# Nearest-neighbour upsampling on one core: the head of the load cut into four DMAs of 32 partitions

## The chip, the cores and the metric

The kernel runs on one core of a Trainium2 chip. The metric is the device time of one execution in microseconds (us). Before the change it is 197.5 us, the median of three runs (197.13 to 197.62). A profile of one execution gives the times of every instruction and, in its trace, of every DMA packet.

## The reference

The input `x` is a float32 tensor of shape 16 x 64 x 64 x 64 (16.78 MB). Each pixel is repeated twice along the rows and twice along the columns, so that the output is 16 x 64 x 128 x 128 (67.11 MB):

```python
for i in range(new_h):
    for j in range(new_w):
        result[:, :, i, j] = x[:, :, i // scale_factor, j // scale_factor].copy()
```

There is no arithmetic. What has to happen is 16.78 MB in and 67.11 MB out, and a fourfold copy in between.

## The kernel before

**Tiling.** The 65,536 rows of 64 floats are dealt out in order to 128 partitions, so that each partition has 512 rows (`R`), which lie in one piece of 128 KB in HBM. One tile, `mem`, holds the whole input (`xt`, 512 rows of each partition) behind a work area of `WF` elements. Partition p holds rows 512p to 512p+511 and writes the output rows that come from them.

**Loads.** Line 194 issues three loads on SyncE's queue (SP), each over all 128 partitions: rows 0 to 255 (64 KB for each partition), rows 256 to 479 (56 KB), and rows 480 to 511 (8 KB). A DMA appears in the trace as one packet for each partition, so 64 KB, 56 KB or 8 KB long, and a semaphore packet of 4 bytes on each of 16 DMA engines at its end. `begin_before_barrier` takes the first `EARLY` SP instructions of the body (they must be loads that wait for nothing) and puts them ahead of SP's part in the barrier that opens the program; with `EARLY = 1` that is the first load. The other two loads follow the barrier.

**Expansion and stores.** `rows` cuts the 512 rows into nine pieces of 40 to 64 rows. For piece n, VectorE (DVE, line 214) expands the first 9/16 of its rows and ScalarE (ACT, line 215) the rest, both with a broadcast access pattern that repeats each element twice and each row twice; line 216 stores the result with one DMA from SP's queue. The first piece has 52 rows, of which DVE takes 29 (128x7424 elements written) and ACT 23 (128x5888). Pieces lie by turns at the bottom of `mem` and just below the rows not yet expanded, so that a later piece overwrites input that has been used up.

**Order.** SP issues everything in program order: three loads, then nine stores. Each store waits for the DVE and ACT copies of its piece. The first store also waits by hand for `loads[-2]`, the last load but one, so that stores begin as the loads end. A copy waits for the load of its rows and for the store that read its place before. DMA semaphores are dealt out in turn from a set of eight, so a later DMA uses a semaphore again after an earlier one. `close_early` (semaphore clearing at line 120) rearranges the end so that only the last store's landing is waited for at the very end.

Of the kernel before, what the change touches and what calls it, by code (L numbers as in the profile page):

```python
# [6 lines left out]

EARLY = 1  # L10


def begin_before_barrier(nc):
# [5 lines left out]
    sp = mybir.EngineType.SP  # L19
    loads = [i for i in body.instructions if i.engine == sp][:EARLY]  # L20
    for load in loads:
# [132 lines left out]
@with_exitstack  # L154
def kernel(
    ctx: ExitStack,
    tc: tile.TileContext,
    x: bass.AP,
    scale_factor: int,
    out: bass.AP,  # L160
):
    nc = tc.nc
    nc.at_finalize(begin_before_barrier)
    nc.at_finalize(close_early)
    P = nc.NUM_PARTITIONS
    s = int(scale_factor)
    B, C, H, W = x.shape
    R = B * C * H // P
    fdt = x.dtype

    xp = x.rearrange("b c h w -> (b c h) w").rearrange("(p r) w -> p r w", p=P)
    op = out.rearrange("b c (h hd) w -> (b c h) (hd w)", hd=s).rearrange(
        "(p r) w -> p r w", p=P
    )

    rows = [52, 40, 52, 63, 52, 64, 63, 63, 63]
    GROW = s * s
    FREE = 79
    WF = FREE * GROW * W
    assert sum(rows) == R
    mem_pool = ctx.enter_context(tc.tile_pool(name="mem", bufs=1))
    mem = mem_pool.tile([P, WF + R * W], fdt, name="mem")
    xt = mem[:, WF:].rearrange("p (r w) -> p r w", r=R)

    cuts = [0, R // 2, R - 32, R]
    loads = [
        nc.sync.dma_start(out=xt[:, lo:hi], in_=xp[:, lo:hi])
        for lo, hi in zip(cuts, cuts[1:])
    ]

    def expanded(r0, r1):
        return (
            xt[:, r0:r1].unsqueeze(2).unsqueeze(4).to_broadcast([P, r1 - r0, s, W, s])  # L200
        )

    r0 = 0
    before = (0, 0)
    for n, k in enumerate(rows):
        size = k * GROW * W
        at = 0 if n % 2 == 0 else WF + r0 * W - size
        assert at >= before[1] or at + size <= before[0]
        before = (at, at + size)
        u = mem[:, at : at + size].rearrange(  # L210
            "p (k a w b) -> p k a w b", k=k, a=s, w=W
        )
        kv = k * 9 // 16
        nc.vector.tensor_copy(out=u[:, :kv], in_=expanded(r0, r0 + kv))  # L214
        nc.scalar.copy(out=u[:, kv:], in_=expanded(r0 + kv, r0 + k))  # L215
        store = nc.sync.dma_start(out=op[:, r0 : r0 + k, :], in_=u)  # L216
        if n == 0:
            tc.add_manual_dep(
                store.ins,
                loads[-2].ins.name,  # L220
                mybir.DependencyInfo(
                    mybir.DependencyClass.Sync, mybir.DependencyReason.DATA
                ),
                reason="stores begin as the loads end",
            )
        r0 += k
# [35 lines left out]
```

## Time and profile before

| what | value |
|---|---|
| median of three runs | 197.5 us (197.13 to 197.62) |
| profiled execution, first to last instruction (span); the profile gives it no other time | 195.8 us |
| between the span and the median | 1.7 us |
| DMA: bytes read and written | 16.78 MB and 67.11 MB, 428 GB/s over the span |
| DVE busy, nine copies | 69.6 us (36%) |
| ACT busy, nine copies and one table load | 51.4 us (26%) |

How to read it: a line of the span in slices gives the busy share of an engine in tenths for equal slices of time; with a window, the 40 slices cover the window. In the DMA view a packet's bytes are counted in the slice in which it begins, so that with long packets a burst in the GB/s row is a set of packets that begin, and the distance between two bursts is the time that one packet takes. The share behind a queue is the time its packets took, as a share of 16 DMA engines. The view of waits names for each instruction line what ended its idle time. Times count from the first instruction, which here is SP's issue of the first load.

### The profile page before, as it was taken

The page shows a single profiled execution, that of the slowest core. Times are in us where ns is not written, and L with a number is a line of the kernel's source. Part 1 is how long each engine was busy: PE and PEld are TensorE (multiplying, and loading weights), DVE is VectorE, ACT ScalarE, POOL GpSimd, SP SyncE. Part 2 cuts the span into 40 slices and gives each one's busy share as a digit, 9 for nine tenths or more (in the row PEclk, how much of TensorE's full clock was granted, in tenths as well). Part 3 has the DMA queues.
Part 4 walks back from the last instruction along what each step waited for, and adds up shares of the span by engine and source line. Part 5 has one row for each costly group of instructions (what it writes and reads, how often), then busy time and mean ns, then how long its engine had stood idle before and what let it go on. Part 6 is the DMA issues. An engine that isn't in the chain of part 4 may idle for free.

```text
span 195.8 us, 102 instructions
## 1 busy us (share of the span) xinstructions
DVE 69.6 (36%) x9; ACT 51.4 (26%) x10; POOL 0.2 (0%) x4
## 2 busy tenths in 40 slices
DVE  0000596000039289069007205930693079100000
ACT  2000558000036083064920005666000074000000
POOL 0000000000000000000000000000000000000000
DMA  9999889699899999999999899999999999999994
GB/s 428 428 428 428 375 375 562 288 462 522 348 442 410 513 402 468 402 422 422 422 422 522 348 522 428 428 428 428 422 422 422 422 422 435 474 488 488 435 422 211
DMA packets 1728, 83.89 MB, mean 428 GB/s; under 512 B 192, under 2 KB 192, under 8 KB 192
## 3 DMA queue, kind: packets, MB, share of 16 engines
q1 hardware_dynamic: 1728, 83.89, 99.3%
HBM read 16.78 MB, written 67.11 MB: 428 GB/s over the span
## 4 chain that ended last, share of the span: by engine, by line
DMA 67%; DVE 18%; issue 0%; DVEq 0%; SPq 0%
DMA out_dram<-mem 48%; DMA mem<-in_x_dram 19%; DVE mem L214 18%; DVEq L214 0%; SPq L216 0%
## 5 line engine op out<-in xcount | busy, mean ns | idle before, releaser
L214 DVE COPY mem<-mem 128x8960 f32<-128x8960 f32 (+3 forms) x9 | 69.6, 7738 | 97.8 <-DMA out_dram<-mem 75.9
L215 ACT COPY mem<-mem 128x7168 f32<-128x7168 f32 (+2 forms) x9 | 50.1, 5572 | 111.7 <-DMA out_dram<-mem 82.7
L215 ACT ACT_TABLE_LOAD x1 | 1.3, 1283 | 0.8 <-PEq L243 0.8
L243 POOL MEMSET const-bfloat16-1.0<- 128x1 bf16 x1 | 0.1, 101 | 0.0
L243 POOL MEMSET const-uint8-127<- 128x1 uint8 x1 | 0.1, 101 | 0.0
L243 POOL MEMSET const-float32-0.0<- 128x1 f32 x1 | 0.1, 98 | 0.2 <-issue 0.2
L243 POOL MEMSET const-float32-1.0<- 128x1 f32 x1 | 0.1, 98 | 0.0
## 6 DMA issues: line engine op xcount, KB each, us to landing
out_dram<-mem SPq DMA_DIRECT2D x4, 8064.0 KB, 28.4
out_dram<-mem SPq DMA_DIRECT2D x3, 6656.0 KB, 19.7
mem<-in_x_dram SPq DMA_DIRECT2D x1, 7168.0 KB, 38.0
out_dram<-mem SPq DMA_DIRECT2D x1, 5120.0 KB, 29.7
mem<-in_x_dram SPq DMA_DIRECT2D x1, 1024.0 KB, 40.1
mem<-in_x_dram SPq DMA_DIRECT2D x1, 21.8
out_dram<-mem SPq DMA_DIRECT2D x1, 29.9
```

Source lines behind the costliest of these rows:

```text
L214: nc.vector.tensor_copy(out=u[:, :kv], in_=expanded(r0, r0 + kv))
L215: nc.scalar.copy(out=u[:, kv:], in_=expanded(r0 + kv, r0 + k))
L243: nc = _bacc.Bacc("TRN2", target_bir_lowering=False, num_devices=1)
```

## The change

The load's first 32 rows of each partition (8 KB) are taken out of the first load and come in four DMAs of their own, each over 32 partitions: partitions 0, 4, 8, ... 124, then 1, 5, ... 125, and so on. The first wide load now has rows 32 to 255 (56 KB for each partition); the two others are as before. `EARLY` goes from 1 to 5, so that the four head loads and the first wide load stand ahead of the barrier. Nothing else is edited; `loads[-2]` still is the wide load of rows 256 to 479. In the changed file the loads are at lines 195 and 198, and the copies and stores at lines 218, 219 and 220.

```diff
-EARLY = 1
+EARLY = 5
...
-    cuts = [0, R // 2, R - 32, R]
+    HEAD, Q = 32, 4
+    cuts = [HEAD, R // 2, R - 32, R]
     loads = [
+        nc.sync.dma_start(out=xt[q::Q, :HEAD], in_=xp[q::Q, :HEAD]) for q in range(Q)
+    ]
+    loads += [
         nc.sync.dma_start(out=xt[:, lo:hi], in_=xp[:, lo:hi])
         for lo, hi in zip(cuts, cuts[1:])
     ]
```

## The prediction

> **What bounds the kernel now.** I read the page's span and DMA queue first, then the chain of waits, then the DMA view in short windows, and last the trace's DMA packets one by one. The page's queue line and its chain:
>
> ```profile
> q1 hardware_dynamic: 1728, 83.89, 99.3%
> ...
> DMA 67%; DVE 18%; issue 0%; DVEq 0%; SPq 0%
> ```
>
> The 16 DMA engines are taken for 99.3% of the span. The 18% that the chain gives to DVE are no idle time of the DMA: while DVE expands a piece, an earlier store is still moving. So the end is set by the bytes, and by the little that is not bytes: 0.7% of 195.8 us, or 1.4 us. It lies at the two ends. The DMA view of the first 5 us and of 10 to 15 us, in slices of 0.125 us:
>
> ```profile
> GB/s 0 0 0 0 0 0 0 0 4194 3146 524 524 0 0 0 0 0 0 0 0 0 0 0 0 0 0 0 0 0 0 0 0 524 2097 2621 1573 1573 0 0 0
> ```
> ```profile
> GB/s 0 0 0 0 0 0 0 0 0 0 1049 1573 2621 2097 1049 0 0 0 0 0 0 0 0 0 0 0 0 0 0 524 1573 2621 1049 2621 0 0 0 0 0 0
> ```
>
> In the first window nothing moves for 1.0 us; then 16 packets of 64 KB begin within four slices, and the next 16 begin about 3 us later. In the second window the distance between two bursts is about 2.4 us. The packets say it exactly. The first load's issue takes 0.383 us on SP. The first packets of the 16 engines begin at 1.009 to 1.478 us and take 3.02 to 3.39 us, so they end at 4.04 to 4.58. From then on each engine runs without a hole: 64 KB packets follow each other every 2.414 us, 56 KB every 2.113, 8 KB every 0.306, and a semaphore packet costs 0.006. From the end of its first packet to its last one each engine needs about 190.9 us. The span's end is therefore the end of the slowest start-up (4.576 us) plus that fixed train, plus some 0.35 us until the last semaphore is seen. **Whatever the change does to the start-up or to the train shifts the time one to one; what it does to DVE, ACT or SP counts only if a store comes late enough to empty the DMA queue.**
>
> **The change, part by part.** The sum is made against the profiled span of 195.8 us; the 1.7 us between it and the median of 197.5 I carry over.
>
> 1. *More packets.* Each engine's eight packets of 64 KB become eight of 8 KB and eight of 56 KB: 0.306 + 2.113 = 2.419 for 2.414 us, 8 x 0.005 = 0.04 us. Seven loads instead of three give four more semaphore packets for each engine: 4 x 0.006 = 0.024 us. Together **+0.06 us** on the path. It is measured on DMAs over 128 partitions; if packets of the narrow DMAs run otherwise, see the second rival.
>
> 2. *When the first packets begin.* A narrow DMA has 32 rows to describe, not 128. The trace has no narrow DMA, so I bound it. If nothing of the 1.478 us goes with the number of rows: 0. If the whole issue (0.383) and the whole spread of the beginnings (1.478 - 1.009 = 0.469) go with it, a quarter stays: -0.75 x 0.852 = -0.64 us for the last engine. Above nothing: the engines would run dry if narrow DMAs came too slowly. One narrow DMA feeds two packets to each engine, 2 x 0.306 + 0.006 = 0.618 us. The loads behind the barrier are issued in 0.332 and 0.424 us, the second 0.383 us after the first; that is faster than they are eaten. The longest distance between two load issues in the trace is 0.79 us (with the barrier between); at that pace 4 x (0.79 - 0.618) = +0.7 us would be lost. Bounds -0.64 to +0.7. The issue rows are all near 0.38 us for 8 KB and for 64 KB alike, so I leave the issue where it is and let half of the spread go: **-0.25 us**.
>
> 3. *How long the first packets take.* They take 0.60 to 0.97 us more than the 2.418 of the later ones. If this is a delay that is paid once whatever the packet's size, the gain is 0. If it goes with the packet's size (first packets run at 71 to 80% of the pace), an 8 KB packet pays an eighth, and 0.53 to 0.85 us are gained. If each of four narrow DMAs paid it again, it would cost up to 3 x 0.97 = 2.9 us; but the row that is nearest, the step from one load to the next on a running engine, shows 0.006 us (a 56 KB packet follows the semaphore packet at once). The train of equal packets after the first speaks for a delay paid once: **0**.
>
> 4. *SP's queue and the barrier.* Four head loads and the wide one are issued ahead of the barrier, and the barrier comes 4 x 0.33 to 4 x 0.42 = 1.3 to 1.7 us later. Behind it stand ACT's table load, the copies, and the last two loads, issued at 0.79 and 1.17 us before. The engines need the next load at about 21.2 us, where the wide load's packets end, so 18 us are spare. Cost 0; without that cover it would be the 1.7 us.
>
> 5. *ACT's table load.* In the built program the table load, which waited for nothing and ran at 0.79 us, now carries waits for three head loads and the wide load, and moves to 21.9 us, where ACT's first copy stood. What is behind it on ACT is the first two copies:
>
> ```profile
> 0.79 1.28 ACT L215 ACT_TABLE_LOAD   x1 [0.79 <-PEq L243]
> 21.86 5.10 ACT L215 COPY mem<-mem 128x5888 f32<-128x5888 f32 x1 [19.79 <-DMA mem<-in_x_dram]
> 21.86 10.89 DVE L214 COPY mem<-mem 128x7424 f32<-128x7424 f32 x2 [21.86 <-DMA mem<-in_x_dram]
> 29.84 4.03 ACT L215 COPY mem<-mem 128x4608 f32<-128x4608 f32 x1 [2.88 <-DVE mem L214]
> 38.86 128.88 SPq L216 DMA_DIRECT2D out_dram<-mem  x9
> ```
>
> The copy ends at 21.9 + 1.28 + 5.1 = 28.3, where ACT idled 2.88 us for DVE until 29.84: hidden. Even with all 1.28 us added to 33.87 there are over 3 us to the first store at 38.86, which waits for the load of rows 256 to 479. Cost 0.
>
> 6. *DVE's first copy.* Its 29 rows lie in the 32 of the head, so in the built program it waits for the four head loads alone and can begin near 5 us instead of 21.9. Nobody gains: the first store still waits for that later load, and DVE's second copy (rows 52 on) for the wide one. Gain 0.
>
> 7. *Stores.* They wait for the same loads; semaphores that are used again belong to DMAs long landed. At 38.8 us the last load (eight packets of 0.306 us on each engine) still runs, so the queue stays full for 2.4 us. Cost 0.
>
> Sum: +0.06 - 0.25 + 0 = -0.19 us; 195.8 becomes 195.6, and 197.5 becomes **197.3 us**. A measurement of this kernel tells some 0.3% (0.6 us) from no change, so the forecast counts as no change.
>
> [...] The trace charges a further DMA on a full queue 0.006 us an engine. [...]
>
> **Rivals.**
>
> *A. The start-up shrinks with the packet (faster).* Term 3 at its lower end. The engine that ends its start-up last (1.478 + 3.098) has 0.68 us of excess; seven eighths are 0.6. With term 2: -0.6 - 0.25 + 0.06 = -0.8 us, **196.7 us**, and 196.3 with term 2 at its end. For it: first packets of 16 engines differ by 0.37 us, as something shared would make them. Against it: the excess does not grow with a later start, and no row shows a short first packet.
>
> *B. The narrow DMAs run at a lower rate (slower).* Their packets may be dealt to the engines in another way than those of wide DMAs, so that two engines meet at one place in the memory and halve each other. Place: the 8 packets of 8 KB at the head. Price: at half rate 8 x 0.306 = +2.45 us; engines that begin 0.15 us apart, about a third of the spread, share only the other half of each packet: 8 x 0.15 = +1.2 us. With terms 1 and 2 about +1.0, **198.5 us**, up to 199.8. It decides once packets after the first take over 0.38 us on average (8 x 0.075 = 0.6 us). For it: no DMA with stepped partitions is in the trace. Against it: in all wide DMAs, loads and stores, all 16 engines hold the same pace.
>
> [...]
>
> *C. The change does not do what it says:* the narrow DMAs use fewer than 16 engines. With eight, those carry 16 packets of 8 KB instead of 8, +2.45 us: **199.7 us**. Nothing in the trace decides it.
>
> **How the numbers follow.** Forecast 0.47, with its own range 196.9 to 197.9 (term 2 from -0.64 to +0.3). A 0.26, B 0.23, C 0.04. So faster 0.26, same 0.47, slower 0.27. The range 196.4 to 199.0 takes in A almost whole and B at its likely price; some 0.06 of A and 0.1 of B and C with the far ends of terms 2 and 3 are left out.
>
> **What would show it.** In the changed profile: first packets of 8 KB that begin at about 1.0 to 1.3 us and take 0.9 to 1.3 us (A: 0.4), later head packets at 0.31 us (B: 0.4 to 0.6), engines without holes between the head loads; DVE's first copy near 5 us; ACT's table load behind the wide load; the first store still just after the load of rows 256 to 479, near 38.7 us. The forecast is wrong if the slowest engine has not moved the eight head packets (8 x 0.306 = 2.45 us of work, as much as the first 64 KB packet that ends at 4.576 us now) between about 4.0 and 4.9 us: earlier speaks for A, later for B or C, and a hole between packets for term 2's upper end.

## The result and the profile after

The changed kernel takes 200.39 us (median of four runs, 199.14 to 201.36) against 197.37 for the kernel before: 1.015 times the time, 95% interval 1.012 to 1.018. The forecast was 197.3 us with a range up to 199.0. The profiled execution took 199.14 us, the shortest of the four; its span is 197.8 us, 2.0 more than before, while the median is 3.0 more. What the longer runs have on top is read below from a second profile of the change.

The page's queue line, its chain, and three of its DMA issue lines (columns: count, KB each, median us from issue to landing):

```profile
q1 hardware_dynamic: 1920, 83.89, 98.8%
...
DMA 66%; DVE 18%; issue 0%; DVEq 0%; SPq 0%
...
out_dram<-mem SPq DMA_DIRECT2D x4, 8064.0 KB, 28.4
...
mem<-in_x_dram SPq DMA_DIRECT2D x2, 7168.0 KB, 29.1
...
mem<-in_x_dram SPq DMA_DIRECT2D x4, 256.0 KB, 3.8
```

The bytes are the same and the DMA still bounds the kernel, but its share falls from 99.3 to 98.8%. A narrow DMA of 256 KB takes 3.8 us to land, though it is 0.6 us of work for 16 engines. The DMA view of the first 5 us, to be laid beside the one of before:

```profile
GB/s 0 0 0 0 0 0 0 0 0 0 393 262 262 0 66 197 459 262 393 459 262 655 328 197 525 131 197 328 262 393 262 131 197 197 328 590 197 1442 131 524
```

Nothing moves for 1.25 us where it was 1.0. With packets this short the row reads as a rate from 2 us on, and its mean up to 4 us lies well below 428 GB/s. By whole microseconds (columns: stretch, length, DVE, ACT and POOL busy, clock, DMA share, GB/s):

```profile
1.00:2.00 1.00, 0.00 (x0) 0.00 (x0) 0.00 (x0) 1.00 0.69 147
2.00:3.00 1.00, 0.00 (x0) 0.00 (x0) 0.00 (x0) 1.00 0.95 377
3.00:4.00 1.00, 0.00 (x0) 0.00 (x0) 0.00 (x0) 1.00 1.08 279
```

From 2 to 4 us, while the head loads run, the engines move 279 to 377 GB/s. The timeline shows what else moved:

```profile
0.00 2.46 SPq L195 DMA_DIRECT2D mem<-in_x_dram  x4
...
2.50 1.91 SPq L198 DMA_DIRECT2D mem<-in_x_dram  x3
6.52 7.88 DVE L218 COPY mem<-mem 128x7424 f32<-128x7424 f32 x1 [6.52 <-DMA mem<-in_x_dram]
23.69 3.09 DVE L218 COPY mem<-mem 128x5632 f32<-128x5632 f32 x1 [9.28 <-DMA mem<-in_x_dram]
23.75 1.28 ACT L219 ACT_TABLE_LOAD   x1 [23.75 <-DMA mem<-in_x_dram]
25.05 9.16 ACT L219 COPY mem<-mem 128x5888 f32<-128x5888 f32 x2
40.69 129.00 SPq L220 DMA_DIRECT2D out_dram<-mem  x9
```

DVE's first copy and the table load stand where they were foreseen in the order, some 1.5 to 1.9 us later than foreseen (6.52 for near 5, 23.75 for 21.9). ACT is done at 34.2 us, and the first store still follows its load, only that it comes at 40.69 instead of 38.86. So 1.83 of the 2.0 us are lost before the first store, in the loads.

**One sum for all runs.** The trace's packets allow an account, as the mean over the 16 engines. A packet does not carry its engine's number; packets are joined to 16 chains by their ends and beginnings. *Begin* is when an engine's first packet begins. *Delay* is what packets of the loads took beyond the fixed length of their size (0.309 us for 8 KB, 2.116 for 56 KB, and so on). *Empty* is the time between an engine's packets in which it had none, up to its first packet of a store. *Stores* is what the store phase took beyond its packets. *Uneven* is how much later than the mean the last engine ends. Together with the *work* (all packets at their fixed pace) and 0.36 us to the end of the span they give the span to 0.04 us in every run, in us:

| run | work | begin | delay | empty | stores | uneven | span |
|---|---|---|---|---|---|---|---|
| before | 193.25 | 1.14 | 0.79 | 0.00 | 0.04 | 0.23 | 195.84 |
| the change | 193.31 | 1.49 | 1.41 | 0.46 | 0.27 | 0.47 | 197.79 |
| the change, again | 193.31 | 1.48 | 1.70 | 1.34 | 0.48 | 0.53 | 199.20 |
| b_early3 | 193.25 | 1.13 | 0.76 | 0.00 | 0.04 | 0.25 | 195.78 |
| m_step4 | 193.31 | 1.27 | 0.69 | 0.04 | 0.45 | 0.35 | 196.48 |
| m_wide | 193.30 | 1.16 | 0.79 | 0.06 | 0.43 | 0.31 | 196.45 |
| m_cont | 193.31 | 1.17 | 3.24 | 0.00 | 0.05 | 0.27 | 198.37 |
| h_wide | 193.30 | 1.15 | 0.66 | 0.01 | 0.10 | 0.50 | 196.08 |
| c_8k | 193.35 | 1.14 | 0.82 | 0.10 | 0.39 | 0.23 | 196.41 |
| h_64 | 193.31 | 1.54 | 1.14 | 0.13 | 0.38 | 0.49 | 197.37 |
| h_128 | 193.32 | 1.50 | 0.68 | 0.04 | 0.35 | 0.44 | 196.70 |
| h_2x64 | 193.30 | 1.47 | 0.76 | 0.24 | 0.47 | 0.42 | 197.02 |
| h_4wide | 193.46 | 1.20 | 0.94 | 0.56 | 0.37 | 0.50 | 197.42 |
| h_cont | 193.31 | 1.23 | 2.48 | 0.04 | 0.05 | 0.20 | 197.69 |
| h_src | 193.31 | 1.46 | 1.44 | 1.49 | 0.50 | 1.05 | 199.60 |

For the change the rise is 0.06 (work) + 0.35 (begin) + 0.62 (delay) + 0.46 (empty) + 0.23 (stores) + 0.24 (uneven) = 1.96 us. In before no engine is ever empty after it has begun. In the change some are: after the 16 beginnings, nine more packets of the head and four 56 KB packets begin on an engine that had nothing queued, and most of them are delayed again, by up to 1.05 us (an 8 KB packet of 1.359 us).

Two of the columns hold more than one thing. Of the delay of 1.41 us in the change, 0.34 is in the 16 first packets and 0.3 to 0.4 in packets that begin on an empty engine; the remaining 0.6 to 0.7 is in packets of the first 10 us that follow another packet without a hole. And *empty* counts two places: the head, and the step from the last load to the first store. In the change nearly all of it is in the head (0.05 at the stores); in its repeat it is 0.62 in the head and 0.72 at the stores, in h_src 0.67 and 0.84, in h_4wide 0.28 and 0.31. In m_step4, m_wide, c_8k and h_128 all but 0.03 at most is at the stores.

### The profile page after: what moved, and what is told of

Same layout as the page of the kernel before. It is cut to its first block, busy times and chain, and to the rows that moved or that the text cites. A ratio compares the mean times of both kernels' runs of the same rounds, so it can differ in the third digit from the quotient of the medians.

```text
span 197.8 us, 111 instructions
## 1 busy us (share of the span) xinstructions
DVE 69.7 (35%) x9; ACT 51.4 (26%) x10; POOL 0.2 (0%) x4
## 3 DMA queue, kind: packets, MB, share of 16 engines
q1 hardware_dynamic: 1920, 83.89, 98.8%
## 4 chain that ended last, share of the span: by engine, by line
DMA 66%; DVE 18%; issue 0%; DVEq 0%; SPq 0%
DMA out_dram<-mem 47%; DMA mem<-in_x_dram 19%; DVE mem L218 18%; DVEq L218 0%; SPq L220 0%
```

## The experiments

The kernels differ from the kernel before or from the change only in the loads. Ratios are against the kernel before on the same chip, with 95% intervals.

**m_step4, m_wide, m_cont: the head in the middle of the queue.** The wide load of rows 32 to 255 goes first (`EARLY = 1`), then the head, then the last two loads:

```diff
+    loads = [nc.sync.dma_start(out=xt[:, HEAD : R // 2], in_=xp[:, HEAD : R // 2])]
+    for q in range(4):                                       # m_step4
+        nc.sync.dma_start(out=xt[q::4, :HEAD], in_=xp[q::4, :HEAD])
...
+    nc.sync.dma_start(out=xt[:, :HEAD], in_=xp[:, :HEAD])    # m_wide, in place of the four
...
+        p = slice(32 * q, 32 * q + 32)                       # m_cont, xt[p] and xp[p] in the four
...
```

> The same seven loads as in the change, but in another order: the wide load of rows 32 to 255 goes first (alone ahead of the barrier, as before the change), the four narrow head loads follow it, then the two last wide loads. So the narrow DMAs are issued while each engine still has some 15 us of queued work. Theory S (supply: the narrow DMAs cost because SP issues them slowly at the start, 0.62 us apart, and the engines begin late and run dry) expects nothing but the 0.06 us of the extra packets: span 195.9 (195.8 to 196.1) and head packets of 0.309 us. Theory P (path: packets of a 32-partition DMA are dealt so that two engines meet at one place and slow each other) expects head packets of 0.4 to 1.4 us here too and a span 1 to 2.5 us longer than before, 196.8 to 198.3.

> As m_step4, but the head is one wide DMA of 8 KB for each of 128 partitions in place of four narrow ones. Control for the cut into more and smaller packets: both theories expect 8 KB packets of 0.309 us and a span of 195.8 to 196.0.

> As m_step4, but each narrow DMA takes 32 neighbouring partitions (0 to 31, 32 to 63, and so on) instead of every fourth. Theory S: nothing, 195.9. Theory P: if the packets are dealt in pairs by their order, neighbouring engines now write neighbouring partitions through the same place all the time, and no packet of theirs can slip past: head packets near twice 0.309 us throughout, span 2 to 2.6 us longer, 197.8 to 198.5.

Measured: m_step4 197.81 us, ratio 1.002 (1.001 to 1.003); m_wide 197.78 us, 1.002 (1.001 to 1.003); m_cont 199.66 us, 1.012 (1.010 to 1.013). The stretches from 19 to 21 us in m_step4, then from 19 to 22 in m_cont:

```profile
19.00:20.00 1.00, 0.00 (x0) 0.00 (x0) 0.00 (x0) 1.00 1.02 426
20.00:21.00 1.00, 0.00 (x0) 0.00 (x0) 0.00 (x0) 1.00 1.04 434
```
```profile
19.00:20.00 1.00, 0.14 (x1) 0.00 (x0) 0.00 (x0) 1.00 1.18 279
20.00:21.00 1.00, 1.00 (x1) 0.00 (x0) 0.00 (x0) 1.00 0.94 197
21.00:22.00 1.00, 1.00 (x1) 0.00 (x0) 0.00 (x0) 1.00 1.10 254
```

With work queued ahead, the stepped narrow DMAs moved at the full rate, 426 to 434 GB/s: all 128 packets of the head in m_step4 took 0.309 us, and m_step4 equals its wide control. Theory P falls for stepped partitions. For neighbouring partitions its price holds: in m_cont the packets fall into two groups, near 0.31 and near 0.6 us, the delay grows by 2.45 us over m_wide, and the head's 1.05 MB take 2.47 + 2.45 = 4.9 us, an estimated 213 GB/s. That two engines meet at one place is only the theory's reason for it; no run shows it. The spans of m_step4 and m_wide were 0.4 us above their expectations; the account puts that into *stores*, which no theory here foresaw.

**h_wide: the head first, but as one DMA** (`EARLY = 2`).

```diff
-        nc.sync.dma_start(out=xt[q::Q, :HEAD], in_=xp[q::Q, :HEAD]) for q in range(Q)
+        nc.sync.dma_start(out=xt[:, :HEAD], in_=xp[:, :HEAD])
```

> The change, but with the head as one wide DMA over 128 partitions in place of four narrow ones (EARLY is 2, so that the wide load of rows 32 to 255 still stands ahead of the barrier). Both theories expect the narrowness to be what costs, so a time near before: span 195.7 to 196.2. If 8 KB packets at the very start or a second issue ahead of the barrier are what costs, it is over 197.

Measured: 197.54 us, ratio 1.001 (1.000 to 1.002), span 196.1. Short packets at the very start and a second issue ahead of the barrier cost almost nothing; the first packets even cost a little less delay (0.66 for 0.79 us). It is the four DMAs.

**h_64, h_src, h_cont and the change again.** In h_64 `HEAD` is 64. In h_cont the partitions are `32 * q` to `32 * q + 31`. In h_src only the source is another:

```diff
+    flat = x.rearrange("b c h w -> (b c h) w").rearrange("(n p r) w -> n p r w", p=32, r=32)
-        nc.sync.dma_start(out=xt[q::Q, :HEAD], in_=xp[q::Q, :HEAD]) for q in range(Q)
+        nc.sync.dma_start(out=xt[q::Q, :HEAD], in_=flat[q]) for q in range(Q)
```

> The change with a head of 64 rows instead of 32: the same four stepped narrow DMAs, of 16 KB packets, and the first wide load that much shorter (48 KB packets). Theory S (supply): one narrow DMA now feeds each engine 1.23 us of work, twice the 0.62 us between two issues, so no engine runs dry after it has begun. What stays is the late first packet (1.3 to 1.9 us) and the first packet's own delay: span 196.0 to 196.5, and hardly any packet after an engine's first one over 0.64 us. Theory P2 (place: stepped narrow packets collide when the engines work in step, as they do at the start and not in the middle of the queue): twice the bytes collide, so at least the loss of the change, span 197.8 to 199.5.

> The change, but each narrow DMA reads one contiguous block of 256 KB of the input instead of 32 rows that lie 512 KB apart; the SBUF side is untouched. So the first 32 rows of each partition hold other data, and the output of those rows is not the reference's. If the slow packets of the change come from where the head is read in HBM, they go: span under 196.8. Theories S and P2 both put the cause elsewhere and expect the time of the change, span 197.5 to 200.

> The change with 32 neighbouring partitions in each narrow DMA instead of every fourth. In the middle of the queue these were issued in 0.35 to 0.43 us (stepped ones 0.53 to 0.61) but half of their packets took twice 0.309 us. So here the first packets should begin near 1.0 us again and no engine should run dry (0.4 us to issue, 0.62 or more to move), and the time should be before plus the 2.4 us that the neighbours cost: span 198.0 to 198.6. If the slow issue were not what makes the first packets late in the change, they begin at 1.3 us or later here too.

> The change once more, unedited: its four runs fell at 199.1, 199.5, 201.3 and 201.4 us, and the profile shows one of the lower ones. Expected 199.0 to 201.5. If this profile is of a longer run, it shows which part of the start-up or of the stores the further 2 us are in: theory S expects them in the head (engines that run dry and start anew), before the first store.

Measured: h_64 198.85 us, ratio 1.009 (1.007 to 1.011); h_src 199.63 us, 1.012 (1.007 to 1.018); h_cont 199.06 us, 1.009 (1.007 to 1.011); the change again 200.55 and 199.59 us, ratio 1.015 (1.012 to 1.017).

h_src is as slow as the change: where the head lies in HBM is not the cause. The repeated change shows what its longer runs are made of: between its two profiles the span grows by 1.41 us, of which 0.88 are empty time and 0.29 delay. Only some 0.2 of the 0.88 are in the head; the rest is at the first store. Before, that store was issued at 38.86 us, while all engines still had packets of the last load; in the repeat one engine began a 56 KB packet only at 7.14 us after 2 to 4 us of nothing, the store had to wait for the latest engine and was issued at 42.25, and 14 of the 16 engines were out of work when its first packets came at 43.1. Before, from 39 to 40 us, and the repeat, from 42 us:

```profile
39.00:40.00 1.00, 0.00 (x0) 0.00 (x0) 0.00 (x0) 1.00 1.04 442
```
```profile
42.00:42.50 0.50, 0.00 (x0) 0.00 (x0) 0.00 (x0) 1.00 0.51 213
42.50:43.00 0.50, 0.00 (x0) 0.00 (x0) 0.00 (x0) 1.00 0.08 33
43.00:43.50 0.50, 0.00 (x0) 0.00 (x0) 0.00 (x0) 1.00 3.70 1556
```

So in the repeat the holes in the head left the engines apart, and a second hole followed near 42 us (0.72 us on the mean). h_cont began at 1.03 us, so the late beginning comes from the stepped shape: its narrow DMAs were issued in 0.39 to 0.42 us, the stepped ones in 0.55 to 0.59. It then lost to its neighbours (delay 2.48) and was hardly ever empty; the time fell 0.3 us under what was expected. h_64 fits neither theory: theory S expected 196.0 to 196.5 and P2 at least 197.8, and it came to 197.37. Of the 1.53 us that its span is over before, 0.40 are in the beginning and 0.35 in delay, 0.34 in the stores, 0.26 in uneven ends and 0.13 empty. Five packets of its third and fourth narrow DMA began on an empty engine, between 4.4 and 6.5 us, where those DMAs had been issued at 1.2 to 2.5. So the pace of the issues is not all: what is issued reaches single engines late.

**c_8k, h_2x64, b_early3: work ahead of the narrow DMAs, more work in each, more issues alone.**

```diff
+    cuts = [2 * HEAD, R // 2, R - 32, R]                                                # c_8k
+    loads = [nc.sync.dma_start(out=xt[:, :HEAD], in_=xp[:, :HEAD])]
+    loads += [nc.sync.dma_start(out=xt[q::Q, HEAD : 2 * HEAD], in_=xp[q::Q, HEAD : 2 * HEAD])
+        for q in range(Q)]                                                              # EARLY = 6
...
-    HEAD, Q = 32, 4
+    HEAD, Q = 32, 2                                                                     # h_2x64, EARLY = 3
...
-EARLY = 1
+EARLY = 3                                                                               # b_early3
```

> The head as one wide DMA of 8 KB packets (2.45 us of work for each engine, issued in 0.37 us), then four stepped narrow DMAs of 8 KB packets for the next 32 rows, then the rest wide; six loads ahead of the barrier. Every narrow DMA is now issued while wide packets are still queued, and each brings 0.62 us of work in 0.62 us. Theory S (supply): the first packets begin at 1.0 us again, no engine runs dry, and the time is that of the wide head plus the extra packets: span 196.0 to 196.5. Theory P2 (stepped narrow packets collide when engines work in step near the start): they collide here too, span 197 or more, with narrow packets well over 0.309 us that begin at once after the one before them.

> The change with two DMAs of 64 partitions (every second one) in place of four of 32: each brings 4 packets of 8 KB, 1.23 us of work for an engine, in one issue, and there are two issues fewer ahead of the wide load. Theory S: about as much supply as the 64-row head but 1.2 us less issuing, so no more loss than that one's 1.5 us: span 196.2 to 197.4. Theory P2: the same bytes through the same stepped pattern, so the loss of the change: 197.8 to 199.5.

> The kernel before with all three wide loads ahead of the barrier (EARLY is 3), nothing else. Tells what the later barrier and more issues at the start cost by themselves: expected nothing, span 195.7 to 196.0, since all that stands behind the barrier has some 18 us to spare. If more issues beside the first packets disturb them, the first packets take over 3.4 us and the span grows.

Measured: c_8k 197.82 us, ratio 1.003 (1.002 to 1.004); h_2x64 197.92 us, 1.003 (1.002 to 1.005); b_early3 197.20 us, 1.000 (0.999 to 1.001). In c_8k, by microseconds:

```profile
2.00:3.00 1.00, 0.00 (x0) 0.00 (x0) 0.00 (x0) 1.00 0.96 401
3.00:4.00 1.00, 0.00 (x0) 0.00 (x0) 0.00 (x0) 1.00 0.98 418
4.00:5.00 1.00, 0.00 (x0) 0.00 (x0) 0.00 (x0) 1.00 1.02 418
5.00:6.00 1.00, 0.00 (x0) 0.00 (x0) 0.00 (x0) 1.00 1.00 418
```

The same four stepped DMAs, issued just as slowly (0.54 to 0.61 us) and run from 3.5 us on, cost next to nothing behind 2.45 us of wide packets: empty 0.10 instead of 0.46 to 1.34, begin 1.14. P2 falls: stepped packets near the start are not slow in themselves (delay 0.82 us, for 0.79 in before). Two DMAs with four packets for each engine lose 0.6 us by the medians, where four with two lose 2.9 to 3.0. In b_early3 the later barrier and two further issues ahead of it cost nothing.

**h_4wide, h_128: shape or too little work.**

```diff
-        nc.sync.dma_start(out=xt[q::Q, :HEAD], in_=xp[q::Q, :HEAD]) for q in range(Q)
+        nc.sync.dma_start(out=xt[:, 8 * q : 8 * q + 8], in_=xp[:, 8 * q : 8 * q + 8]) for q in range(Q)  # h_4wide
...
-    HEAD, Q = 32, 4
+    HEAD, Q = 128, 4                                                                                      # h_128
```

> The head again in four DMAs and five loads ahead of the barrier, but each of the four is over all 128 partitions and 8 rows deep (2 KB packets, eight for each engine and DMA, at least 0.6 us of work). If the narrow, stepped shape is what delivers late (a wide DMA was issued in 0.37 to 0.42 us, a stepped one in 0.55 to 0.59), this one begins at 1.0 us and runs without holes: span 196.0 to 197.0, with a little for the 24 further packets on each engine. If four small DMAs in a row at the start are too little work whatever their shape, engines run dry here too: span 197.5 to 199.5.

> The change with a head of 128 rows: four stepped narrow DMAs of 32 KB packets, 2.45 us of work for each engine and DMA against 0.62 us between issues. With 64 rows some engines still ran dry, as packets of the fourth DMA began up to 4.7 us after its issue. Late delivery expects that 2.45 us of work covers this: empty time of the engines under 0.1 us on the mean, about 0.8 us of delay in the first packets, the late beginning at 1.3 to 1.9 us left over: span 196.3 to 196.9. If stepped narrow packets are slow in themselves near the start, four times the bytes of the change are slow: span 198 or more.

Measured: h_4wide 199.05 us, ratio 1.009 (1.006 to 1.013); h_128 197.92 us, 1.003 (1.002 to 1.004). The first microseconds of h_4wide:

```profile
1.00:2.00 1.00, 0.00 (x0) 0.00 (x0) 0.00 (x0) 1.00 0.81 248
2.00:3.00 1.00, 0.00 (x0) 0.00 (x0) 0.00 (x0) 1.00 0.96 342
3.00:4.00 1.00, 0.00 (x0) 0.00 (x0) 0.00 (x0) 1.00 1.15 348
```

It begins at 1.0 us and is issued every 0.42 to 0.47 us, faster than its 0.65 us of work for each DMA, and yet its engines are empty for 0.56 us (0.28 in the head) and move 342 to 348 GB/s. Its span, 197.42, is just under the range for engines that run dry. So the stepped shape makes the beginning late (1.46 to 1.54 us on the mean with four of them at the head, 1.20 here), but four small DMAs in a row at the start are too little work for wide ones too. Here the packets are also only 2 KB long, and no run tells that from the size of the DMA. h_128 came out as late delivery expects: 2.45 us of work for each DMA leaves 0.04 us empty and no packet of its loads but the first 16 on an empty engine. With 32, 64 and 128 rows in the head, empty and delay together fall from 1.87 (3.04 in the repeat) over 1.27 to 0.72 us, less than the 0.79 of before. What stays is the late beginning (1.50), with 0.35 in the stores and 0.44 in uneven ends.

No version here beats the kernel before.

## Why the prediction was wrong

1. *More packets, +0.06:* held. Work grows by 0.064 us, and in m_step4 the loads lose nothing else in sum that its control does not.
2. *When the first packets begin, -0.25:* wrong in sign; +0.35 was measured. I took the issue row of wide DMAs (0.38 us); a stepped one takes 0.55 to 0.59 us and its first packet begins at 1.33, not 1.01. **The step that failed is the sentence that issues are "faster than they are eaten".** They came every 0.61 to 0.64 us for 0.618 us of work, and the engines were empty for 0.46 us, 1.34 in the repeat. And the comparison itself was too simple, since h_4wide is issued faster than it is eaten and still runs empty: a mean pace does not tell when a single engine gets its packets. The end that I kept for this, +0.7, counted the empty time only, not the delay that engines paid when they began anew (up to 1.05 us).
3. *The first packet's delay, 0:* part of rival A is real, as 8 KB first packets were delayed by 0.34 us on the mean in the change, for 0.79 with 64 KB. But engines that ran empty paid again, packets that followed one another without a hole were slow as well, and the sum rose to 1.41 and 1.70. **The second step that failed:** I had a bound for paying again (up to 2.9 us) and dropped it for the step between two loads on a running engine. That row shows a full queue; the change makes a short or empty one, so it was not the nearest. The term stood at 0 and measured +0.62, in the repeat +0.91.
4. *Barrier, table load, DVE's first copy:* held at no cost, as the timeline and b_early3 show.
5. *Stores:* their order held. The cover of 2.4 us by the last load held nearly in the first profile (0.05 us empty) and not in the repeat (0.72), as it counted on engines that keep together; the sum had no term for engines that drift apart, and the uneven ends alone cost +0.24. The stores' packets also ran a little slower, 0.27 to 0.48 us in sum for 0.04 before. It comes with several variants (m_wide among them, which has no narrow DMA) and not with others (m_cont, h_cont). What sets it stays open.

Rival B had the right side, though 200.39 us is over its upper end of 199.8. The half rate that it priced was measured for neighbouring partitions (m_cont, packets near 0.6 us), not for every fourth (m_step4, 0.309 us); that two engines meet at one place in the memory, its reason, was not shown. Its mark, head packets over 0.38 us on the mean after the first ones, was met (0.40, and 0.42 in the repeat) for another reason: stepped packets with more work queued, in c_8k and h_128, are not slow, and h_4wide, with no narrow DMA, has 0.9 us of delay behind its first packets. Rival C is out: 256 semaphore packets for 16 DMAs are 16 engines each.

I priced a further DMA by a row of a full queue, 0.006 us an engine. In m_step4 and c_8k the row is right (0.04 and 0.10 us empty). At the head of an empty queue four DMAs cost begin, delay and empty of 1.4 to 2.6 us more than one wide load, 0.4 to 0.6 us for each. No run here shows the reason.

What is shown: in the change engines ran empty (0.46 us, 1.34 in the repeat) and mostly began anew with a delay (up to 1.05 us); the repeat lost again at the first store (0.72 us empty); more work in each DMA (h_128, 0.04 us empty, 0.68 delay) or work ahead of them (c_8k, 0.10 and 0.82) removed the holes in the head and the further delay; stepped partitions by themselves (m_step4, ratio 1.002), HBM addresses (h_src, as slow as the change at 199.63 us) and the barrier (b_early3, 1.000) did not cause them. What is only argued: that late and uneven delivery of packets to the engines is behind it. No view here shows a packet on its way between issue and engine. Why packets without a hole before them are slow in a short queue, 0.6 to 0.7 us in sum, stays open too.

## What to carry to other kernels

When DMA bounds a kernel, its first load should be one that gives every engine enough work until the next DMA has reached all of them. Here 2.45 us sufficed (c_8k, h_128) and 1.23 did not (h_64, h_2x64). Four small loads cut out of it left holes (0.46 us empty in the change, 1.34 in the repeat) that nothing hid: the spans grew by 2.0 and 3.4 us. Read the cost of a further DMA from a row with the same queue: what costs 0.006 us on a full one cost up to 0.6 us on an empty one. And where a change opens a stream, count every new beginning, not the first alone.

## What the runs showed of the hardware

- A DMA over stepped partitions was issued in 0.53 to 0.66 us (every fourth) or 0.57 to 0.58 (every second), and the wide load right behind one in 0.58 to 0.61. In kernels without stepped DMAs the loads, over neighbouring partitions or all 128, were issued in 0.33 to 0.53, most of them in 0.33 to 0.43.
- DMAs over 32 neighbouring partitions ran at half the rate, an estimated 213 GB/s from 1.05 MB in 2.47 + 2.45 us (m_cont); those over every fourth ran at 426 to 434 GB/s (m_step4).
- The delay of an engine's first packet, 0.5 to 1.0 us with 64 KB packets (before, b_early3), did not vanish with 8 KB ones (0 to 0.8 us in h_wide and the change). It came again for most packets that began on an empty engine (up to 1.05 us in the change).
